# A two-block network on one core: cumulative sums in fp32r and a 512-column output product in the gated mixer

## The chip, the cores and the metric

The kernel runs on one core of a Trainium2 chip. Its engines work side by side, each through its own list of instructions in order, and wait for each other through semaphores: PE (TensorE) multiplies matrices into banks of PSUM, and PEld is its weight load, which overlaps the products; DVE (VectorE) and ACT (ScalarE) do elementwise work; POOL (GpSimd) does a little of it; SP issues the transfers. The metric is the device time of one execution in microseconds (us). The clock granted to TensorE in the profiled execution was 0.998 of full speed on average.

## The reference

`reference` runs a first block of two layers (three kinds of attention, a merge and a layer norm) on an activation of 256 tokens and 1024 features, then a second block of two layers. A layer of the second block is a gated feed-forward network, the mixer, and another feed-forward network, each behind a normalisation and with a gated residual. All is in float32. The mixer has three branches (retention, stick-breaking attention with four heads, and a state-space model) and one output product. What the change touches is this:

```
z = einsum('bhtd,bhsd->bhts', qb, kb) * scale
visible = s_pos[None, :] < t_pos[:, None]
log_beta = log_sigmoid(z)
log_keep = where(visible, log_sigmoid(-z), 0.0)
tail = cumsum(log_keep, axis=3, reverse=True) - log_keep
w = where(visible, exp(log_beta + tail), 0.0)
...
mixed = concatenate([y_ret, y_sb, y_ssm], axis=-1) @ w_out[l]     # 1536 x 1024
h = h + (1.0 + mod[:, :, 5]) * mixed
```

## The kernel before

Activations are kept with features on the 128 partitions and the 256 tokens along the row, so one feature tile is 128x256. Weights stream in as 128x1024 tiles (`raw`), through transfers that SP issues in one fixed sequence. Nearly every product keeps float32 accuracy by splitting both operands into a high and a low fp32r part. For a weight ACT makes the high part `wh` (L383) and DVE the low part `wl` (L384). For an activation ACT makes the high half (L492) and DVE the low half (L493) of one `pair` tile, which holds both side by side as 512 columns. There are two ways of adding up one 128-row step of a product:

- `mm3` (L394, L395, L396): three products of 256 columns, high weight by high half, high weight by low half, low weight by high half, all into the same 256 columns of a bank.
- `mm2` (L401, L402): the high weight over the whole pair, 512 columns, and the low weight over the high half into the second 256 columns. The result lies in two halves that have to be added when it is read.

`mm2` is used in the feed-forward down product, `mm3` in most of the rest, the mixer's output product among it.

The mixer runs twice (mixer 0 about 865 to 1045 us, mixer 1 about 1420 to 1605 us). Two of its parts matter here.

Stick-breaking: for each of the four heads, `b1` forms scores (L1814, L1815) and from them on ACT (Abs L1842, then Exp and Ln) and DVE (L1845, L1846, L1847) the logs of keeping, `k`, a 128x384 tile of type `fs`. `b2` multiplies `k` by a triangle of ones (`tri`, L1820 to L1822) to get the cumulative sums. These are plain fp32 products. DVE subtracts (L1856), ACT takes the exponential, DVE masks (L1858), and `b3` multiplies by the values. `pipeline(4, b1, b2, b3)` staggers the heads, and the pieces are mixed as side work between the `mm3` steps of the projections. A sibling of `tri`, `tri2` (L1828, L1830), takes a high and a low part as fp32r and is used by the state-space branch. Scores and cumulative sums share the two `sc` banks.

Output product: eight output tiles n of 128 features, each the sum of 12 `mm3` steps, four per branch: `YB` (stick-breaking), `YS` (state space), `YR` (retention). For n = 0 to 3 the YB and YS steps are side by side with the other branches' tails, and the YR steps come last. For n = 4 to 7 (`wide`, then `part`) the order is written out by hand (`inorder`), for the rest a scheduler orders the instructions when the program is built. `done(n)` (`resid`) then adds the tile into the residual on DVE (L1603, one instruction for every 256 columns of the bank), and `early` prepares the next normalisation: ACT makes the high half (L1495), DVE the low half (L1496), ACT the square (L1489), POOL adds the squares up (L1385). At the end PE sums the squares over the partitions (L542) inside the first product of the feed-forward network (`modhead`, 258 columns). The bank pool `mm` has four banks, and a bank of n = 0 to 3 has to be read out before `wide(4)` can write to it.

## Time and profile before

| | |
|---|---|
| time, median of 3 runs | 1797.98 us (1797.68 to 1798.31) |
| the profiled execution, its own time | 1798.37 us |
| its span, first to last instruction | 1796.6 us |
| PE busy | 1767.8 us, 98% |
| PEld busy | 1647.3 us, 92% |
| DVE busy | 1462.6 us, 81% |
| ACT busy | 1100.5 us, 61% |
| POOL busy | 190.3 us, 11% |
| share of the 16 DMA engines | 59.9% |

Shares of busy time are averages over the whole span. Products are pipelined on PE: the next starts before the one before it has ended, so what one costs is the distance from its start to the next start, not its duration. A row of the timeline gives start, duration, engine, line, operation, output and inputs; idle time ahead of it stands in brackets with the instruction that ended it.

### The profile page before, as it was taken

How to read it: one execution, taken by the hardware profiler on the slowest of the kernel's cores; microseconds unless marked ns; L12 is line 12 of the kernel's file. 1: busy time of each engine (PE TensorE's matmuls, PEld its weight loads, DVE VectorE, ACT ScalarE, POOL GpSimd, SP SyncE). 2: the span in 40 equal slices, each digit the busy share in tenths (PEclk: the TensorE clock that was granted, in tenths of full speed). 3: DMA queues.
4: the chain of work that ended last, by engine and by line, in shares of the span. 5: the costliest groups of instructions: out<-in, count | busy, mean ns of one | idle time of the engine just before them, and what ended most of it. 6: DMA issues, size and time to landing. Idle time of an engine off the chain costs nothing.

```text
span 1796.6 us, 32910 instructions
## 1 busy us (share of the span) xinstructions
PE 1767.8 (98%) x12720; PEld 1647.3 (92%) x12720; DVE 1462.6 (81%) x2893; ACT 1100.5 (61%) x2178; POOL 190.3 (11%) x205
## 2 busy tenths in 40 slices
PE   8999999999999999999999999999999999999997
PEld 8988999998899999988998998889888999899886
DVE  6787778898778789887797789697978798989774
ACT  6676555678655468674565665556555566566543
POOL 1000021300001120001114110011000104110001
PEclk9999999999999999999999999999999999999999
DMA  8755566455556655547545458585867554857761
GB/s 309 268 219 201 194 246 244 164 201 202 190 208 234 241 182 202 186 174 270 187 154 205 147 202 314 196 303 183 303 243 273 193 187 171 309 207 284 258 251 51
DMA packets 57758, 393.22 MB, mean 219 GB/s; under 512 B 6401, under 2 KB 7041, under 8 KB 15361
## 3 DMA queue, kind: packets, MB, share of 16 engines
q1 hardware_dynamic: 57600, 391.11, 59.9%
q8 instruction: 100, 1.64, 0.3%
q14 instruction: 58, 0.47, 0.1%
HBM read 390.04 MB, written 1.05 MB: 218 GB/s over the span
## 4 chain that ended last, share of the span: by engine, by line
PE 84%; DVE 8%; ACT 3%; issue 2%; DMA 2%; POOL 1%; SPq 0%; POOLq 0%; ACTq 0%; DVEq 0%
PE mm L401 21%; PE mm L394 14%; PE mm L395 14%; PE mm L396 14%; PE mm L402 11%; DVE wl L384 3%; DMA raw<-in_w 2%; DVE raw L345 2%; PE mm L445 1%; PE mm L446 1%; PE mm L447 1%; ACT wh L383 1%; PE tp L626 1%; POOL act L1395 1%; PE sc L599 0%
## 5 line engine op out<-in xcount | busy, mean ns | idle before, releaser
L383 ACT ACTIVATE wh<-raw 128x1024 fp32r<-128x1024 f32 (+2 forms) x585 | 603.0, 1036 | 446.2 <-PE mm L395 177.2
L384 DVE TENSOR_TENSOR wl<-raw,wh 128x1024 fp32r<-128x1024 f32 (+2 forms) x585 | 702.7, 1208 | 190.2 <-ACT wh L383 188.8
L394 PE MATMUL mm<-pair,wh 128*128 128x256 f32 (+2 forms) x2666 | 764.5, 287 | 6.3 <-ACT wh L383 5.2
L395 PE MATMUL mm<-pair,wh 128*128 128x256 f32 (+2 forms) x2666 | 752.6, 283 | 0.9 <-DVE pair L493 0.9
L396 PE MATMUL mm<-pair,wl 128*128 128x256 f32 (+2 forms) x2666 | 751.3, 282 | 1.0 <-DVE wl L384 0.9
L401 PE MATMUL mm<-pair,wh 128*128 128x512 f32 x1626 | 569.1, 394 | 0.0
L394 PEld LDWEIGHTS mm<-pair,wh 128*128 128x128 f32 x2666 | 504.2, 189 | 12.2 <-ACT wh L383 5.5
L395 PEld LDWEIGHTS mm<-pair,wh 128*128 128x128 f32 x2666 | 505.5, 190 | 1.8 <-DVE pair L493 1.3
L396 PEld LDWEIGHTS mm<-pair,wl 128*128 128x128 f32 x2666 | 504.9, 189 | 1.8 <-DVE wl L384 1.8
L402 PE MATMUL mm<-pair,wl 128*128 128x256 f32 x1626 | 455.6, 280 | 0.0
L401 PEld LDWEIGHTS mm<-pair,wh 128*128 128x128 f32 x1626 | 305.3, 188 | 70.9
L402 PEld LDWEIGHTS mm<-pair,wl 128*128 128x128 f32 x1626 | 306.2, 188 | 0.0
L345 DVE SCALAR_TENSOR_TENSOR raw<-raw,cond 128x1024 f32<-128x1024 f32 x160 | 194.6, 1227 | 18.0 <-DMA raw<-in_w 17.8
L1382 POOL TENSOR_TENSOR act<-act 128x256 f32<-128x256 f32 x9 | 10.8, 1200 | 563.7 <-ACT act L1489 496.6
L492 ACT ACTIVATE pair<-act 128x256 fp32r<-128x256 f32 x130 | 52.8, 411 | 27.2 <-DVE act L1673 11.7
L1385 POOL TENSOR_TENSOR act<-act 128x256 f32<-128x256 f32 x52 | 44.4, 858 | 181.3 <-ACT act L1489 172.3
L493 DVE TENSOR_TENSOR pair<-act,pair 128x256 fp32r<-128x256 f32 x130 | 56.6, 440 | 6.5 <-ACT pair L492 6.5
L304 ACT ACTIVATE fs<-fs,small 128x128 f32<-128x128 f32 x96 | 42.9, 448 | 25.6 <-DVE small L578 25.4
L445 PE MATMUL mm<-wh,pair 128*128 128x512 f32 x136 | 55.5, 408 | 0.1
L1649 DVE TENSOR_TENSOR act<-act,mm 128x256 f32<-128x256 f32 x118 | 48.8, 414 | 6.1 <-ACT act L1648 6.1
L446 PE MATMUL mm<-wl,pair 128*128 128x512 f32 x136 | 53.6, 394 | 0.0
L447 PE MATMUL mm<-wh,pair 128*128 128x512 f32 x136 | 53.6, 394 | 0.0
(304 smaller groups left out, 1686.2 us busy)
## 6 DMA issues: line engine op xcount, KB each, us to landing
raw<-in_w SPq DMA_DIRECT2D x329, 1024.0 KB, 4.8
raw<-in_w SPq DMA_DIRECT2D x32, 896.0 KB, 5.4
raw<-in_w SPq DMA_DIRECT2D x10, 512.0 KB, 4.1
tab_moba<-in_t SPq DMA_DIRECT2D x1, 1536.0 KB, 10.4
raw<-in_w SPq DMA_DIRECT2D x2, 768.0 KB, 4.8
raw<-in_w SPq DMA_DIRECT2D x3, 384.0 KB, 4.8
vt<-in_x SPq DMA_DIRECT2D x4, 256.0 KB, 6.7
out<-pair SPq DMA_DIRECT2D x4, 256.0 KB, 2.1
```

The source lines that it names most:

```text
L345: self.V.scalar_tensor_tensor(r, r, 0.5, self.cond, op0=ALU.mult, op1=ALU.mult, accum_out=self.adar[:, self.ada_n : self.ada_n + 1],)
L383: self.A.activation(h[:, :w], r, AF.Copy)
L384: self.V.tensor_tensor(l[:, :w], r, h[:, :w].bitcast(F32), op=ALU.subtract)
L394: T.matmul(ps, wh, x[0], start=first, stop=False)
L395: T.matmul(ps, wh, x[1], start=False, stop=False)
L396: self.pe = T.matmul(ps, wl, x[0], start=False, stop=last)
L401: T.matmul(ps, wh, x[2], start=first, stop=False)
L402: self.pe = T.matmul(ps[:, S:], wl, x[0], start=False, stop=last)
L445: T.matmul(ps, X[k][0][:, t], h[:, c], start=k == 0, stop=False)
L446: T.matmul(ps, X[k][0][:, t], l[:, c], start=False, stop=False)
L447: T.matmul(ps, X[k][1][:, t], h[:, c], start=False, stop=k == nk - 1)
L493: self.V.tensor_tensor(l, src, h.bitcast(F32), op=ALU.subtract)
```

## The change

Two edits in `mixer`.

In stick-breaking `tri` is gone. `b1` makes two more `fs` tiles for each head: ACT copies `k` to fp32r (`kh`), DVE subtracts it from `k` (`kl`), and `b2` calls `tri2` with the two: two products of 384 columns and two of 128, in fp32r.

In the output product `mm3` is replaced by `mm2` in `part` and in `wide`, so each tile n uses a whole bank of 512 columns, and `done` reads it with two L1603 instead of one.

In the changed kernel the lines from `tri` on have other numbers: `tri2` is L1821 and L1823, the two new instructions are L1842 (ACT) and L1843 (DVE), L1845, L1846, L1847 become L1838, L1839, L1840, L1856 and L1858 become L1852 and L1854, and L1883 becomes L1879. Lines up to L1814 keep theirs.

```diff
--- before.py
+++ after.py
@@ -1815,13 +1815,6 @@
             T.matmul(ps[:, S:384], k[:, P:S], q[:, P:S], start=True, stop=True)
             return ps[:, :384]
 
-        def tri(rhs):
-            ps = self.scb()
-            T.matmul(ps[:, S:384], self.trig, rhs[:, S:384], start=True, stop=True)
-            T.matmul(ps[:, 0:S], self.trig, rhs[:, 0:S], start=True, stop=False)
-            T.matmul(ps[:, P:S], self.ones, rhs[:, S:384], start=False, stop=True)
-            return ps[:, :384]
-
         def tri2(rs):
             ps = self.scb()
             for i, r in enumerate(rs):
@@ -1845,14 +1838,17 @@
                 V.scalar_tensor_tensor(k, z, 0.0, a, op0=ALU.max, op1=ALU.add)
                 V.scalar_tensor_tensor(a, z, 0.0, a, op0=ALU.min, op1=ALU.subtract)
                 V.tensor_tensor(k, k, LT, op=ALU.mult)
-                sbst[hh] = (a, k)
+                kh, kl = (self.fp.tile([P, 384], F32R, name="fs") for _ in range(2))
+                A.activation(kh, k, AF.Copy)
+                V.tensor_tensor(kl, k, kh.bitcast(F32), op=ALU.subtract)
+                sbst[hh] = (a, (kh, kl))
 
             return f
 
         def b2(hh):
             def f():
                 a, k = sbst.pop(hh)
-                tl = tri(k)
+                tl = tri2(k)
                 V.tensor_tensor(a, a, tl, op=ALU.subtract)
                 self.lut("ln", a, a, AF.Exp)
                 V.tensor_tensor(a, a, LT, op=ALU.mult)
@@ -2058,23 +2054,23 @@
         def part(n, Y, first=False, last=False):
             def f():
                 if first:
-                    pp[n] = self.bank()[:, :S]
+                    pp[n] = self.bank()
                 if n % 2 == 0:
                     uu[n // 2] = gen.take()
                 wh, wl = uu[n // 2]
                 for k in range(4):
                     c = slice((n % 2 * 4 + k) * P, (n % 2 * 4 + k + 1) * P)
-                    self.mm3(pp[n], wh[:, c], wl[:, c], Y[k], first and k == 0, last and k == 3)
+                    self.mm2(pp[n], wh[:, c], wl[:, c], Y[k], first and k == 0, last and k == 3)
 
             return f
 
         def wide(n):
             wh, wl = gen.take()
-            pp[n] = self.bank()[:, :S]
+            pp[n] = self.bank()
             Y2 = YB + YS
             for k in range(8):
                 c = slice(k * P, k * P + P)
-                self.mm3(pp[n], wh[:, c], wl[:, c], Y2[k], k == 0, False)
+                self.mm2(pp[n], wh[:, c], wl[:, c], Y2[k], k == 0, False)
 
         mix([part(n, YB, True) for n in range(4)], early)
         mix([part(n, YS) for n in range(4)], side[1:])
```

The change moves instructions. On PE, at the first head of stick-breaking in mixer 0, before:

```order
L396 MATMUL mm<-pair,wl 128x256
L1820 MATMUL sc<-fs,t_94 128x128
L1821 MATMUL sc<-fs,t_94 128x256
L1822 MATMUL sc<-fs,t_94 128x128
L394 MATMUL mm<-pair,wh 128x256
L395 MATMUL mm<-pair,wh 128x256
L396 MATMUL mm<-pair,wl 128x256
L1814 MATMUL sc<-pair 128x256
L1815 MATMUL sc<-pair 128x128
L394 MATMUL mm<-pair,wh 128x256
L395 MATMUL mm<-pair,wh 128x256
```

and of the changed kernel:

```order
L396 MATMUL mm<-pair,wl 128x256
L1821 MATMUL sc<-fs,tr 128x384 x2
L1823 MATMUL sc<-fs,tr 128x128 x2
L394 MATMUL mm<-pair,wh 128x256
L395 MATMUL mm<-pair,wh 128x256
L396 MATMUL mm<-pair,wl 128x256
L394 MATMUL mm<-pair,wh 128x256
L395 MATMUL mm<-pair,wh 128x256
L396 MATMUL mm<-pair,wl 128x256
L394 MATMUL mm<-pair,wh 128x256
L1814 MATMUL sc<-pair 128x256
L1815 MATMUL sc<-pair 128x128
L395 MATMUL mm<-pair,wh 128x256
```

The three fp32 products have become four fp32r products (two and two), and the next head's scores (L1814) come seven products after them instead of three.

On DVE, at the same head (`wl` is the low half of a streamed weight, L1883 and L1879 belong to the rotary tiles of the retention branch), before:

```order
L1845 SCALAR_TENSOR_TENSOR fs<-sc,fs 128x384
L1846 SCALAR_TENSOR_TENSOR fs<-sc,fs 128x384
L1847 TENSOR_TENSOR fs<-fs,tab_lt 128x384
L384 TENSOR_TENSOR wl<-raw,wh 128x1024
L1883 SCALAR_TENSOR_TENSOR pair<-fs,vt,pair 128x256
L1845 SCALAR_TENSOR_TENSOR fs<-sc,fs 128x384
L1883 SCALAR_TENSOR_TENSOR pair<-fs,vt,pair 128x256
L1846 SCALAR_TENSOR_TENSOR fs<-sc,fs 128x384
L1883 SCALAR_TENSOR_TENSOR pair<-fs,vt,pair 128x256
L1847 TENSOR_TENSOR fs<-fs,tab_lt 128x384
L1883 SCALAR_TENSOR_TENSOR pair<-fs,vt,pair 128x256
L1856 TENSOR_TENSOR fs<-fs,sc 128x384
```

and of the changed kernel:

```order
L1838 SCALAR_TENSOR_TENSOR fs<-sc,fs 128x384
L1839 SCALAR_TENSOR_TENSOR fs<-sc,fs 128x384
L1840 TENSOR_TENSOR fs<-fs,tab_lt 128x384
L384 TENSOR_TENSOR wl<-raw,wh 128x1024
L1843 TENSOR_TENSOR fs<-fs 128x384
L1879 SCALAR_TENSOR_TENSOR pair<-fs,vt,pair 128x256 x2
L1852 TENSOR_TENSOR fs<-fs,sc 128x384
L1879 SCALAR_TENSOR_TENSOR pair<-fs,vt,pair 128x256
L384 TENSOR_TENSOR wl<-raw,wh 128x1024
L1838 SCALAR_TENSOR_TENSOR fs<-sc,fs 128x384
L1854 TENSOR_TENSOR fs<-fs,tab_lt 128x384
L1839 SCALAR_TENSOR_TENSOR fs<-sc,fs 128x384
```

The low part of `k` (L1843) stands behind a `wl` of 128x1024, and the next head's first step (L1838) now comes behind this head's L1852; before it came ahead of it.

On DVE, from the last low half of the retention tiles to the readout of tile 4, in mixer 1, before:

```order
L493 TENSOR_TENSOR pair<-act,pair 128x256
L1603 SCALAR_TENSOR_TENSOR act<-mm,mod,act 128x256 x4
L1496 SCALAR_TENSOR_TENSOR pair<-act,mod,pair 128x256
L384 TENSOR_TENSOR wl<-raw,wh 128x1024
L1496 SCALAR_TENSOR_TENSOR pair<-act,mod,pair 128x256 x3
L384 TENSOR_TENSOR wl<-raw,wh 128x1024 x2
L1603 SCALAR_TENSOR_TENSOR act<-mm,mod,act 128x256
```

and of the changed kernel:

```order
L493 TENSOR_TENSOR pair<-act,pair 128x256
L1603 SCALAR_TENSOR_TENSOR act<-mm,mod,act 128x256 x6
L1496 SCALAR_TENSOR_TENSOR pair<-act,mod,pair 128x256
L1603 SCALAR_TENSOR_TENSOR act<-mm,mod,act 128x256
L1496 SCALAR_TENSOR_TENSOR pair<-act,mod,pair 128x256
L1603 SCALAR_TENSOR_TENSOR act<-mm,mod,act 128x256
L1496 SCALAR_TENSOR_TENSOR pair<-act,mod,pair 128x256
L384 TENSOR_TENSOR wl<-raw,wh 128x1024
L1496 SCALAR_TENSOR_TENSOR pair<-act,mod,pair 128x256
L384 TENSOR_TENSOR wl<-raw,wh 128x1024 x2
L1603 SCALAR_TENSOR_TENSOR act<-mm,mod,act 128x256 x2
```

The readout of tiles 0 to 3 has grown from four L1603 to eight, six of them ahead of anything else, and that of tile 4 from one to two.

## Rows read from the trace of the kernel before

**Rows 1.** The page: busy time of the engines, and the chain that ended last.
```profile
PE 1767.8 (98%) x12720; PEld 1647.3 (92%) x12720; DVE 1462.6 (81%) x2893; ACT 1100.5 (61%) x2178; POOL 190.3 (11%) x205
...
PE 84%; DVE 8%; ACT 3%; issue 2%; DMA 2%; POOL 1%; SPq 0%; POOLq 0%; ACTq 0%; DVEq 0%
```

**Rows 2.** The page, costliest groups: count, busy us, mean ns of one.
```profile
L394 PE MATMUL mm<-pair,wh 128*128 128x256 f32 (+2 forms) x2666 | 764.5, 287 | 6.3 <-ACT wh L383 5.2
...
L401 PE MATMUL mm<-pair,wh 128*128 128x512 f32 x1626 | 569.1, 394 | 0.0
...
L402 PE MATMUL mm<-pair,wl 128*128 128x256 f32 x1626 | 455.6, 280 | 0.0
```

**Rows 3.** Windows of mixer 0 and 1: busy us of each engine, clock, DMA share, GB/s.
```profile
897.00:935.00 38.00, 37.94 (x303) 37.13 (x302) 34.98 (x64) 25.59 (x49) 1.25 (x6) 1.00 0.45 158
...
1530.00:1560.00 30.00, 29.03 (x239) 27.85 (x238) 30.00 (x82) 14.98 (x43) 2.48 (x3) 1.00 0.94 358
```

**Rows 4.** Timeline of PE, cumulative sums of one head: start us, duration, instruction.
```profile
905.66 0.38 PE L1820 MATMUL sc<-fs,t 128*128 128x128 f32 x2
...
906.66 0.28 PE L395 MATMUL mm<-pair,wh 128*128 128x256 f32 x1
```

**Rows 5.** Timeline of PE, `tri2` in the state-space branch of mixer 0.
```profile
971.63 0.51 PE L1828 MATMUL sc<-fs,tr 128*128 128x384 f32 x2
...
972.33 0.28 PE L395 MATMUL mm<-pair,wh 128*128 128x256 f32 x1
```

**Rows 6.** Timeline of PE, first and last of 20 `mm3` steps in the output product.
```profile
1004.51 0.28 PE L394 MATMUL mm<-pair,wh 128*128 128x256 f32 x1
...
1011.21 0.28 PE L394 MATMUL mm<-pair,wh 128*128 128x256 f32 x1
```

**Rows 7.** Timeline of PE, `mm2` steps in the feed-forward down product, 22 steps apart.
```profile
807.12 0.40 PE L401 MATMUL mm<-pair,wh 128*128 128x512 f32 x1
807.36 0.28 PE L402 MATMUL mm<-pair,wl 128*128 128x256 f32 x1
...
814.80 0.40 PE L401 MATMUL mm<-pair,wh 128*128 128x512 f32 x1
```

**Rows 8.** Timeline of DVE at the head of rows 4.
```profile
903.48 0.55 DVE L1847 TENSOR_TENSOR fs<-fs,tab_lt 128x384 f32<-128x384 f32 x1
903.95 1.22 DVE L384 TENSOR_TENSOR wl<-raw,wh 128x1024 fp32r<-128x1024 f32 x1
905.08 0.48 DVE L1883 SCALAR_TENSOR_TENSOR pair<-fs,vt,pair 128x256 f32<-128x256 f32 x1
```

**Rows 9.** Timeline of ACT at the same head.
```profile
903.92 0.49 ACT L1842 ACTIVATE fs<-sc 128x384 f32<-128x384 f32 x1
```

**Rows 10.** Timeline of DVE, end of the output product in mixer 1.
```profile
1578.19 0.42 DVE L493 TENSOR_TENSOR pair<-act,pair 128x256 fp32r<-128x256 f32 x1
1579.20 1.66 DVE L1603 SCALAR_TENSOR_TENSOR act<-mm,mod,act 128x256 f32<-128x256 f32 x4 [0.59 <-PE mm L396]
...
1587.34 0.47 DVE L1603 SCALAR_TENSOR_TENSOR act<-mm,mod,act 128x256 f32<-128x256 f32 x1
...
1598.84 0.48 DVE L1603 SCALAR_TENSOR_TENSOR act<-mm,mod,act 128x256 f32<-128x256 f32 x1
```

**Rows 11.** Timeline of PE there: first product of `wide(4)`, and the sum of squares.
```profile
1579.74 0.39 PE L394 MATMUL mm<-pair,wh 128*128 128x256 f32 x1
...
1601.84 0.28 PE L542 MATMUL tp<-t,act 128*128 128x1 f32 x2
```

**Rows 12.** Timeline of POOL: last sum of squares of mixer 0 and of mixer 1.
```profile
1040.68 0.73 POOL L1385 TENSOR_TENSOR act<-act 128x256 f32<-128x256 f32 x1 [3.17 <-ACT act L1489]
...
1600.31 0.74 POOL L1385 TENSOR_TENSOR act<-act 128x256 f32<-128x256 f32 x1 [2.72 <-ACT act L1489]
```

**Rows 13.** Timeline of PE: the sum of squares over the partitions in mixer 0.
```profile
1043.29 0.28 PE L542 MATMUL tp<-t,act 128*128 128x1 f32 x2
```

## Prediction

> **What bounds the kernel now.** I read the page first: its busy line and chain [rows 1] show that PE works 98% of the span and makes up 84% of the chain that ended last, DVE 8%. An edit is therefore worth what it takes from PE, until PE starts to wait. The windows of the two mixers came next, since all that changes lies there: from 897 to 935 us, where mixer 0 does its stick-breaking, PE is busy 37.94 of 38.00 us with DVE at 34.98; in mixer 1, from 1530 to 1560 us, DVE is busy in all 30.00 us, the DMA engines 0.94 of the time, and PE only 29.03 [rows 3]. The clock is at its upper level (2.4 GHz) in both. So mixer 0 passes on what PE saves, while mixer 1 has a stretch between stick-breaking and output product in which DVE and the transfers may swallow it. Last I read the timelines of PE, DVE, ACT and POOL around the edits for prices and slack [rows 4 to 13], and the order of the changed kernel for what stands behind what.
>
> **The cumulative sums.** Before, `tri` starts at 905.66 and the second product behind it at 906.66 [rows 4]; taking off one ordinary distance of 0.12 us, the three fp32 products cost 0.88 us. `tri2`, which the state-space branch already uses at the same size, goes from 971.63 to 972.33 [rows 5], less 0.12 is 0.58 us. So 0.30 us for each of eight heads, 2.4 us of PE. In mixer 0 I let all 1.2 us count. In mixer 1 it may be lost in the stretch at 1530 us: between 0 and -1.2 us, and I take -0.6, since neither end has a row that favours it.
>
> What is added is on other engines: for each head a copy on ACT (0.49 us, by the same size in rows 9), hidden because ACT is busy 25.59 of 38.00 us there, and a subtraction on DVE, 0.47 us by the distance of L1847 to its successor [rows 8], 3.8 us for eight heads. DVE has 3.02 us free in that window, so four of them (1.9 us) fit on the sum; whether they fit in time depends on the place. By the order of the changed kernel the low part of `k` stands behind one `wl`. For the head of rows 4: L1847 ends at 904.03, `wl` holds DVE from 903.95 to 905.08, the subtraction would run from there to 905.63, and PE reaches the sums at 905.66. That is just in time. For the other three heads the distances are as short or a little shorter, because the next head's first step now stands behind this head's L1852: I put 0.1 us of PE wait on each, +0.3 us in each mixer, +0.6 together. The ends are 0 (cover as above) and one whole `wl`, 1.13 us, on each of eight heads, +9.0; I take a value near the lower end because the head for which there are rows lies at it. What is queued behind the waiting product on PE are `mm3` steps, which nobody needs at once, and then the next scores, whose result heads the next head's chain.
>
> **The output product.** By durations, `mm3` is three products of 0.28 to 0.29 us and `mm2` one of 0.394 and one of 0.280 [rows 2], 0.18 us less. But products are pipelined. In the output product itself 19 `mm3` steps take 1011.21 - 1004.51 = 6.70 us, 0.3526 each [rows 6]; in the down product 22 `mm2` steps take 814.80 - 807.12 = 7.68 us, 0.3491 each [rows 7]. Both move 768 columns. The saving is 0.0035 us a step, and with 8 tiles of 12 steps in two mixers, 192 steps, it is -0.7 us.
>
> The Trainium skill, TensorE: Matmul & The Clock Gate, section Back-to-back issue gap, gives a sustained 131 ns for a product of 512 columns in a stream with weight loads. Rows 7 disagree: L401 to L402 is 0.24 us. By the page the saving would be about 0.11 x 192 = 21 us (an estimate); by the row it is what stands above.
>
> **The readout of tiles 0 to 3.** A bank now holds two halves, and so 16 more L1603 run on DVE, at 0.41 us each (1.66 us for four, [rows 10]), 6.6 us. Before, in mixer 1, the last low half L493 ends at 1578.61, the first L1603 starts at 1579.20, ends at about 1579.68, and `wide(4)` starts at 1579.74 [rows 10, 11]: PE already waits for the first readout. Now the first product of a step reads both halves of the pair, so no work on the last quarter starts before L493 is through, and the bank of tile 0 is free only after its second L1603, which comes third in DVE's order (both tiles' first halves ahead): 1579.20 + 2 x 0.41 + 0.48 = 1580.50, and `wide(4)` at 1580.56. That is +0.8 us. In mixer 0 nothing waits at this place in the trace before, and the same wait may appear in part: between 0 and +0.8, I take +0.3.
>
> **The readout of tiles 4 to 7.** Here DVE and ACT work in a loop: L1603, high half, square, next `wh`, next `wl`, next L1603. In mixer 1 it goes from 1587.34 to 1598.84 in three rounds [rows 10], later than PE needs it, and its end is POOL's sum, 1600.31 to 1601.05, for which PE's L542 at 1601.84 does not wait: 0.79 us of slack [rows 11, 12]. One more L1603 in each of four tiles puts 4 x 0.41 = 1.64 us on the loop. The four extra L1603 of tiles 0 to 3 lie ahead of it, between 1579.20 and 1587.34: 8.14 us, in which DVE does four L1603 (0.41), four L1496 (0.40, as L1603) and three `wl` (1.13), 6.6 us in all. So 1.5 us are free and take in most of the other 1.64; I leave 0.5 of it. The sum comes 2.1 us later, and the slack is 0.79 and the 0.8 that `wide(4)` has lost: PE waits about 0.6 us for L542 (0 if less arrives late, 1.7 if all 3.28 do). In mixer 0 the slack is 1043.29 - 1041.41 = 1.88 us [rows 12, 13] and about 0.3 more: 2.1 - 2.2 is nothing, the upper end is 3.28 - 1.88 = 1.4, and I take +0.2.
>
> **The sum.** -1.2 - 0.6 + 0.6 - 0.7 + 0.8 + 0.3 + 0.6 + 0.2 = 0.0 us. Against the profiled execution (span 1796.6 us and 1.8 around it, 1798.37) that gives 1798.4; this execution is 0.4 above the median, so against the median the forecast is 1798.0 us: no change that can be measured (the bound is about 0.2%, 3.6 us).
>
> **Rivals.** First, PE's gain stays and the tails are hidden: the scheduler's order leaves the readouts enough room. -2.4 - 0.7 = -3.1 us, 1794.9. For it speaks mixer 0, where nothing waits at the end of the output product; against it mixer 1, where PE waits for DVE at that place already.
>
> Second, a 512-column product costs less than its columns where it stands beside the mixer's short ones, so the durations count: 0.18 x 192 = 35 us, about 1763. Rows 2 speak for it, rows 6 and 7 against it, and those are starts, which is what PE pays.
>
> Third, the other side: DVE's queue sets the pace in stick-breaking. The place is the low part of `k` behind a `wl`; it decides once that `wl` starts later than about 1.6 us ahead of PE's sums (1.13 for itself and 0.47 for the subtraction). Then each head pays up to 1.13 us: if all eight do, 9.0 - 2.4 - 0.7 + 1.9 for the tails = +7.8, 1805.8; if five do, 5.6 in place of 9.0, +4.4, 1802.4. For it speaks DVE's 34.98 of 38.00 us [rows 3] and that heads now follow each other strictly; against it that the head of rows 4 and 8 arrives in time. The Trainium skill, VectorE: DVE Perf Modes, section Rules for kernel authors, says to minimise the count of DVE operations; the change adds 24, and no run here shows yet what they cost. By that rule the change would lose.
>
> **How the numbers follow.** The forecast has a chance of 0.62, the first rival 0.19, the second 0.05, the third 0.14. The forecast's own range takes in the ends of its terms: with all of mixer 1's gain, no waits at the heads, nothing in mixer 0's tail and none at mixer 1's L542, -2.3 us; with no gain in mixer 1, the wait for `wide(4)` whole in mixer 0 too, and L542 at 1.4 and 1.7, +3.4 us. That is 1795.7 to 1801.4. The first rival and the near part of the third widen it to 1794.5 to 1802.0. Faster by over 0.2% (below 1794.4): the second rival, less than half of the first, a little of the forecast, 0.16. Slower by over 0.2% (above 1801.6): most of the third and the upper end of the forecast, 0.14. Within 0.2%: 0.70.
>
> **What would show it.** Right: the cumulative sums take 0.58 us from start to the next ordinary product, with no or short idle time ahead of the low part's product; the mixer's steps lie 0.349 us apart; a new wait of PE for L1603 at the start of `wide(4)` in mixer 1, and for L1385 or L542's input at its end; DVE's busy time up by about 10 us with the span the same. Wrong: idle time of PE for L1843 at several heads (third rival), L401 in the mixer much under 0.23 us ahead of L402 (second), or no new wait in either tail (first). A change of more than 4 us with none of these would mean that transfers moved, which I have left out because SP's list is the same in both kernels.

## The result, and the profile after

The changed kernel takes 1807.55 us (median of 4 runs, 1805.71 to 1811.43) against 1798.14 (1797.68 to 1798.76) before: 9.4 us slower, a ratio of 1.0052 with a 95% interval of 1.0041 to 1.0064. I had forecast 1798.0 and no measurable change. The profiled execution took 1808.32 us with a span of 1806.5, and a mean granted clock of 0.994 against 0.998.

The page of the changed kernel, busy time and chain, answers to [rows 1]:

```profile
PE 1771.7 (98%) x12512; PEld 1640.1 (91%) x12512; DVE 1474.0 (82%) x2917; ACT 1102.3 (61%) x2186; POOL 193.9 (11%) x205
...
PE 81%; DVE 10%; ACT 3%; issue 3%; DMA 2%; POOL 1%; POOLq 0%; DVEq 0%; ACTq 0%
```

DVE has 11.4 us more to do, where I had about 10, and so far nothing is alarming. The chain is not the same: PE's part has fallen from 84% to 81%, DVE's has risen from 8% to 10%. The list of PE's waits in both mixers (850 to 1625 us) says where:

```profile
PE sc L1821 <- POOL fs L1935: 3.7, 2, 1.9
PE tp L542 <- POOL act L1385: 3.2, 2, 1.6
PE mm L401 <- DVE pair L493: 1.9, 1, 1.9
PE tp L1403 <- DVE small L554: 1.1, 1, 1.1
PE tp L617 <- DVE fs L1854: 0.6, 2, 0.3
PE mm L401 <- DVE act L1603: 0.4, 1, 0.4
```

Columns: who waited for whom, us in total, times, the longest. Before, the second and third did not exist, and the first was shorter:

```profile
PE sc L1828 <- POOL fs L1939: 1.3, 2, 0.7
```

To see which wait reaches the end I cut both executions at the same instructions, starts of PE's sums of squares L542: the one ahead of each mixer, the one that opens its output product, the one ahead of the feed-forward network behind it, and the last of the program. The lengths of the pieces:

| piece, us | before | after | difference |
|---|---|---|---|
| start to mixer 0 | 862.52 | 861.80 | -0.7 |
| M0: mixer 0, projections and branches | 137.29 | 138.14 | +0.9 |
| O0: mixer 0, output product | 43.48 | 44.83 | +1.4 |
| F0: feed-forward networks between | 373.39 | 373.47 | +0.1 |
| M1: mixer 1, projections and branches | 137.20 | 138.63 | +1.4 |
| O1: mixer 1, output product | 47.96 | 52.94 | +5.0 |
| F1: last feed-forward network | 183.08 | 184.69 | +1.6 |
| rest | 11.7 | 12.0 | +0.3 |

The first row is code that both kernels share: mixer 0 begins between 860.4 and 866.2 us in the fourteen profiles, so times inside a mixer have to be counted from its start. Four things are in this table.

**The gain on the sums never leaves the branches.** The edit itself does what it should; PE at the head that answers to [rows 4]:

```profile
904.93 0.51 PE L1821 MATMUL sc<-fs,tr 128*128 128x384 f32 x2
905.28 0.33 PE L1823 MATMUL sc<-fs,tr 128*128 128x128 f32 x2
905.45 0.33 PE L394 MATMUL mm<-pair,wh 128*128 128x256 f32 x1
905.62 0.28 PE L395 MATMUL mm<-pair,wh 128*128 128x256 f32 x1
```

From 904.93 to 905.62, less an ordinary distance of 0.12, is 0.57 us, and no idle time: the subtraction was ready, as forecast. But PE then waits at the state-space branch, whose first sums want what POOL makes. Before:

```profile
959.26 0.33 PE L1830 MATMUL sc<-fs,tr 128*128 128x128 f32 x2
960.27 0.62 PE L1828 MATMUL sc<-fs,tr 128*128 128x384 f32 x2 [0.68 <-POOL fs L1939]
```

and after:

```profile
957.83 0.51 PE L1821 MATMUL sc<-fs,tr 128*128 128x384 f32 x2
958.18 0.33 PE L1823 MATMUL sc<-fs,tr 128*128 128x128 f32 x2
960.41 0.62 PE L1821 MATMUL sc<-fs,tr 128*128 128x384 f32 x2 [1.90 <-POOL fs L1935]
```

Counted from the start of the mixer (862.52 before, 861.80 after), the product ahead of the wait starts at 96.74 and at 96.38, so PE is 0.36 us earlier; the one behind it starts at 97.75 and at 98.61, 0.86 us later, and that is the +0.9 of M0. Of the 1.2 us saved, 0.3 had gone before, into a new wait for a head's mask (the line of L1854 above). The wait of 0.68 us was in the trace of before, at the very place that the gain had to pass, and I did not price it.

**The doubled readout delays the sum of squares in both mixers.** DVE at the end of the output product of mixer 1, which answers to [rows 10]:

```profile
1584.36 2.44 DVE L1603 SCALAR_TENSOR_TENSOR act<-mm,mod,act 128x256 f32<-128x256 f32 x6 [0.71 <-PE mm L402]
...
1593.98 0.99 DVE L1603 SCALAR_TENSOR_TENSOR act<-mm,mod,act 128x256 f32<-128x256 f32 x2
...
1607.04 1.00 DVE L1603 SCALAR_TENSOR_TENSOR act<-mm,mod,act 128x256 f32<-128x256 f32 x2
```

From the first readout to that of tile 4 it is 9.62 us (8.14 before), and the three rounds from tile 4 to tile 7 take 13.06 us (11.50 before). Two L1603 on one tile take 0.99 us, so the second starts 0.52 us behind the first, more than the 0.41 of four independent ones. POOL's last sum at that place, for [rows 12]:

```profile
1609.03 0.73 POOL L1385 TENSOR_TENSOR act<-act 128x256 f32<-128x256 f32 x1 [3.23 <-ACT act L1489]
```

and PE's sum of squares behind it, for [rows 11]:

```profile
1609.81 0.38 PE L542 MATMUL tp<-t,act 128*128 128x1 f32 x2 [1.59 <-POOL act L1385]
```

The sum ends at 1609.76 and PE, ready 1.59 us earlier, starts 0.05 later. Before, it started 0.79 us behind POOL's end without having waited [rows 11, 12].

**PE waits for the whole pair of the first retention tile.** Before, it began with the high half and waited twice, 0.5 and 0.7 us. Now it stands still from the transposes to the end of L493, 1.94 us (the bracket at the end of the second row):

```profile
1574.75 0.91 PE L1436 MATMUL tp<-t,act 128*128 128x128 f32 x3
1577.60 0.80 PE L401 MATMUL mm<-pair,wh 128*128 128x512 f32 x1 [1.94 <-DVE pair L493]
```

**The clock falls.** This I had not thought of at all. Windows of the changed kernel, mixer 1 (the granted clock is the third number from the end, 1.00 is 2.4 GHz):

```profile
1560.00:1565.00 5.00, 4.70 (x21) 4.28 (x22) 4.79 (x31) 3.01 (x13) 0.00 (x0) 0.66 0.63 216
1575.00:1580.00 5.00, 3.06 (x11) 2.31 (x11) 4.02 (x8) 3.23 (x8) 0.00 (x0) 0.74 0.97 380
1605.00:1610.00 5.00, 3.29 (x26) 3.02 (x25) 2.72 (x5) 2.63 (x4) 1.46 (x2) 1.00 0.53 197
1610.00:1615.00 5.00, 5.00 (x30) 5.00 (x30) 4.67 (x20) 2.00 (x2) 0.00 (x0) 0.66 0.27 111
```

Each low stretch lies at a standstill of PE: 1.1 us ahead of L1403 at 1560.3, 1.9 us ahead of 1577.60, 1.6 us ahead of 1609.81. In it the products of 258 columns start 0.22 us apart, where they did 0.12:

```profile
1611.61 0.42 PE L395 MATMUL mm<-pair,wh 128*128 128x258 f32 x1
1611.83 0.42 PE L396 MATMUL mm<-pair,wl 128*128 128x258 f32 x1
```

The last stretch, a mean of 0.66 over its 5 us and so some 3.4 us at half clock, is the whole +1.6 us of F1: nothing else in that feed-forward network has changed. The Trainium skill, TensorE: Matmul & The Clock Gate, section HAM oscillation — how this bites in real kernels, tells of standstills of PE, after which the array runs at half its clock. The trace agrees with the order of events, but the page's rule is for longer standstills than the 1.1 to 1.9 us here, and there the trace decides. Before, the profile of these stretches shows 1.00 throughout.

### The profile page after: what moved, and what is told of

Same layout as the page of the kernel before. It is cut to its first block, busy times and chain, and to the rows that moved or that the text cites. A ratio compares the mean times of both kernels' runs of the same rounds, so it can differ in the third digit from the quotient of the medians.

```text
span 1806.5 us, 32511 instructions
## 1 busy us (share of the span) xinstructions
PE 1771.7 (98%) x12512; PEld 1640.1 (91%) x12512; DVE 1474.0 (82%) x2917; ACT 1102.3 (61%) x2186; POOL 193.9 (11%) x205
## 4 chain that ended last, share of the span: by engine, by line
PE 81%; DVE 10%; ACT 3%; issue 3%; DMA 2%; POOL 1%; POOLq 0%; DVEq 0%; ACTq 0%
PE mm L401 22%; PE mm L394 13%; PE mm L395 13%; PE mm L396 13%; PE mm L402 11%; DVE wl L384 4%; DMA raw<-in_w 2%; ACT wh L383 1%; PE mm L445 1%; PE mm L446 1%; PE mm L447 1%; DVE raw L345 1%; PE tp L626 1%; DVE act L1603 1%; PE sc L599 0%
## 5 line engine op out<-in xcount | busy, mean ns | idle before, releaser
L394 PE MATMUL mm<-pair,wh 128*128 128x256 f32 (+2 forms) x2474 | 711.2, 287 | 5.2 <-ACT wh L383 4.6
L395 PE MATMUL mm<-pair,wh 128*128 128x256 f32 (+2 forms) x2474 | 699.4, 283 | 0.1
L396 PE MATMUL mm<-pair,wl 128*128 128x256 f32 (+2 forms) x2474 | 698.4, 282 | 0.3 <-DVE wl L384 0.2
L401 PE MATMUL mm<-pair,wh 128*128 128x512 f32 x1818 | 639.7, 396 | 2.3 <-DVE pair L493 1.9
L402 PE MATMUL mm<-pair,wl 128*128 128x256 f32 x1818 | 510.5, 281 | 0.4 <-DVE wl L384 0.4
L394 PEld LDWEIGHTS mm<-pair,wh 128*128 128x128 f32 x2474 | 468.9, 190 | 10.8 <-ACT wh L383 4.7
L395 PEld LDWEIGHTS mm<-pair,wh 128*128 128x128 f32 x2474 | 469.8, 190 | 0.8 <-DVE pair L1496 0.3
L401 PEld LDWEIGHTS mm<-pair,wh 128*128 128x128 f32 x1818 | 342.5, 188 | 81.7 <-DVE pair L493 2.3
L1385 POOL TENSOR_TENSOR act<-act 128x256 f32<-128x256 f32 x52 | 44.4, 859 | 183.1 <-ACT act L1489 174.2
L493 DVE TENSOR_TENSOR pair<-act,pair 128x256 fp32r<-128x256 f32 x130 | 56.9, 442 | 6.7 <-ACT pair L492 6.7
L445 PE MATMUL mm<-wh,pair 128*128 128x512 f32 x136 | 55.4, 408 | 0.1
L1603 DVE SCALAR_TENSOR_TENSOR act<-mm,mod,act 128x256 f32<-128x256 f32 x95 | 44.1, 479 | 12.4 <-PE mm L396 6.8
```

Source lines behind the costliest of these rows:

```text
L394: T.matmul(ps, wh, x[0], start=first, stop=False)
L395: T.matmul(ps, wh, x[1], start=False, stop=False)
L396: self.pe = T.matmul(ps, wl, x[0], start=False, stop=last)
L401: T.matmul(ps, wh, x[2], start=first, stop=False)
L402: self.pe = T.matmul(ps[:, S:], wl, x[0], start=False, stop=last)
L445: T.matmul(ps, X[k][0][:, t], h[:, c], start=k == 0, stop=False)
```

## The experiments

All times are against the kernel before, timed beside each of them on the same chip (1798.1 us beside the changed kernel, 1798.6 to 1799.1 beside the others). The pieces of the profiled execution:

| kernel | median us | ratio (95%) | M0 | O0 | F0 | M1 | O1 | F1 |
|---|---|---|---|---|---|---|---|---|
| before | | | 137.3 | 43.5 | 373.4 | 137.2 | 48.0 | 183.1 |
| changed | 1807.55 | 1.0052 (1.0041 to 1.0064) | 138.1 | 44.8 | 373.5 | 138.6 | 52.9 | 184.7 |
| `tri_only` | 1800.72 | 1.0015 (1.0006 to 1.0023) | 138.1 | 43.5 | 373.4 | 139.5* | 47.9 | 183.1 |
| `mm2_only` | 1804.92 | 1.0033 (1.0021 to 1.0045) | 137.2 | 44.8 | 375.0* | 137.2 | 52.3* | 183.2 |
| `mm2_tiles03` | 1799.38 | 1.0002 (0.9994 to 1.0011) | 137.3 | 43.2 | 373.4 | 137.3 | 50.9** | 183.1 |
| `mm2_tiles47` | 1800.39 | 1.0008 (0.9999 to 1.0017) | 137.3 | 43.4 | 373.4 | 137.2 | 49.5 | 184.7* |
| `tri_nokl` | 1799.02 | 1.0003 (0.9993 to 1.0012) | 137.0 | 43.4 | 373.4 | 137.4 | 48.4 | 183.1 |
| `tri_pool` | 1806.01 | 1.0041 (1.0027 to 1.0055) | 140.6 | 43.4 | 373.4 | 142.5 | 48.4 | 183.1 |
| `hifirst` | 1807.99 | 1.0053 (1.0038 to 1.0068) | 139.6* | 44.6 | 375.0* | 138.1 | 51.8* | 183.2 |
| `q7` | 1804.72 | 1.0029 (1.0016 to 1.0042) | 139.5* | 43.1 | 374.4 | 138.1 | 49.7 | 184.1 |
| `read_twice` | 1802.43 | 1.0020 (1.0010 to 1.0029) | 137.3 | 44.1 | 373.5 | 137.9 | 50.9 | 184.7* |
| `sub_alone` | 1802.66 | 1.0020 (1.0010 to 1.0029) | 140.2* | 43.4 | 373.4 | 140.2* | 47.0 | 183.1 |
| `masks` | 1798.19 | 0.9998 (0.9989 to 1.0008) | 137.2 | 43.5 | 373.4 | 137.9 | 48.5 | 183.1 |
| `fill` | 1805.72 | 1.0035 (1.0021 to 1.0049) | 139.5* | 44.8 | 373.5 | 138.1 | 50.9 | 183.2 |

A star is a stretch of low clock in that piece (two in O1 and one in F1 of the changed kernel, which is left unmarked). With no star a piece repeats within 0.1 us in M0 and O0 and within 0.2 in F1, so that single profiles can be compared there; M1 and O1 repeat less well: where the code is that of before, from 137.2 to 137.9 and from 47.0 to 48.5. In `q7` the cut lies at the first of four sums of squares, so some 0.9 us of its O0 and O1 stand in the next piece; its mixer 1 is also ordered otherwise, without the wait at the state-space branch.

**One edit at a time.** `tri_only` leaves the output product as it was, `mm2_only` the sums:

```diff
-                    self.mm2(pp[n], wh[:, c], wl[:, c], Y[k], first and k == 0, last and k == 3)
+                    self.mm3(pp[n], wh[:, c], wl[:, c], Y[k], first and k == 0, last and k == 3)
```

> Only the cumulative sums are changed; the output product keeps three products of 256 columns. Theory A (the gain of 0.30 us a head is lost at the state-space branch, whose first cumulative sums wait for POOL at the end of a chain through DVE and POOL, and DVE has 1.9 us more to do in each mixer ahead of it): about 1.0 us later at the end of mixer 0's branches and 1.4 us in mixer 1, 1799.5 to 1801, with PE's wait for POOL there at 1.5 to 1.9 us in each mixer against 0.7 and 0.6 before, and no other new wait. Theory B (the sums save PE what was forecast, all of the loss is in the output product): 1796 to 1797.5.

> Only the output product is changed, in all eight tiles; the cumulative sums stay in fp32. Theory A (the waits at the end of the output product and the clock that falls behind them make 7 of the 9.4 us): 1803.5 to 1807, with PE waiting 1 to 1.6 us for POOL ahead of the sum of squares in each mixer, about 1.9 us for the low half of a retention tile in mixer 1, and the granted clock under 1 in mixer 1 behind at least one of them. Theory B (the output product is all of the loss): 1807 to 1810.

Both came out as theory A has it. The sums alone cost +0.15% (2.7 us), with POOL's wait at 1.9 and 1.8 us; the output product alone +0.33% (5.9 us). Together that is 8.6 us of the 9.4. So neither edit gains anything, and the sums, on which the forecast rested, lose.

**Which part of the sums.** `sub_alone` adds the copy and the subtraction to the kernel before and uses neither; `tri_nokl` has the fp32r products and leaves the subtraction out (the low part of `k` is replaced by the high part, and each head has one `fs` tile less); `masks` takes DVE work away from the kernel before.

```diff
# sub_alone, on the kernel before
+                kh, kl = (self.fp.tile([P, 384], F32R, name="fs") for _ in range(2))
+                A.activation(kh, k, AF.Copy)
+                V.tensor_tensor(kl, k, kh.bitcast(F32), op=ALU.subtract)
                 sbst[hh] = (a, k)
# tri_nokl, on tri_only
-                V.tensor_tensor(kl, k, kh.bitcast(F32), op=ALU.subtract)
-                sbst[hh] = (a, (kh, kl))
+                sbst[hh] = (a, (kh, kh))
# masks, on the kernel before (dg: columns 0 to 127 and 256 to 383); the second mask of a head alike
-                V.tensor_tensor(k, k, LT, op=ALU.mult)
+                V.tensor_tensor(dg(k), dg(k), dg(LT), op=ALU.mult)
```

> The kernel before with two instructions a head added, the copy of k to fp32r on ACT and the subtraction on DVE, whose results nothing uses: the sums stay three fp32 products, so PE saves nothing. Theory A (DVE's load delays the chain to POOL on which the state-space branch waits): PE waits there as long as PE would be early, about 0.8 to 1.8 us in each mixer against 0.7 and 0.6 before, and the branch starts at the same time as in the kernel with the edit: 1799.5 to 1801.5. Theory D (the order of the heads, which only the fp32r sums force, delays it): 1798 to 1799.

> Only the cumulative sums are changed, and the low part of k is left out: tri2 takes the high part twice, so PE does the same four fp32r products, DVE loses the eight subtractions and each head one fs tile. Theory A (the subtraction on DVE, 0.47 us a head, delays the chain through DVE and POOL on which the state-space branch waits): the wait of PE for POOL stays but ends earlier, by most of 4 x 0.47 = 1.9 us in each mixer; 1796.5 to 1798.5. Theory D (not DVE's load, but the changed order of heads and steps delays that chain): as the kernel with the low part on DVE, 1799.5 to 1801.

> The kernel before, but the two mask products of each head in stick-breaking leave out the middle 128 of 384 columns, where the mask is 1: DVE does 256 columns in place of 384, sixteen times, about 0.1 us less each. If DVE's load ahead of the state-space branch is what PE waits for (theory A), PE's wait for POOL of 0.7 and 0.6 us shrinks and the time falls by 0.3 to 1.3 us: 1797 to 1798.3 against 1798.3 to 1799. If not (theory D), no change.

The wait for POOL, the one line of PE's waits (850 to 1625 us), of `sub_alone`:

```profile
PE sc L1828 <- POOL fs L1942: 3.7, 2, 1.9
```

and of `tri_nokl`:

```profile
PE sc L1821 <- POOL fs L1934: 2.4, 2, 1.2
```

The copy and the subtraction alone, with nothing saved on PE, lengthen the wait from 1.3 to 3.7 us and cost 0.20% (a little above the range of its expectation, by two stretches of low clock in its profile). With the copy and without the subtraction the wait is 2.4 us, and 1799.02 us lies between the ranges of the two theories, no different from before. Counted from the start of mixer 0, the state-space sums begin behind the wait at 97.75 us before, 97.43 in `tri_nokl`, 98.58 in `tri_only` and 99.25 in `sub_alone`. So DVE's subtraction puts 1.15 us (98.58 against 97.43) on the chain that ends at POOL, and the copy is not the cause. Of the 1.2 us that PE saves in mixer 0, 0.55 go into the longer wait for POOL, 0.27 into a new one at a head's scores (L1814), until DVE has read the `sc` bank, and 0.3 arrive (M0 is 137.0 against 137.3), too little to be seen in ten runs. Since a scheduler orders DVE's list anew in each kernel, what the subtraction takes and how it reorders the rest are not separated.

`masks` is a miss for theory A in its simple form: with DVE relieved, the wait stays at 1.3 us and the time does not move by what can be measured (its interval is 0.9989 to 1.0008). So DVE's load does not by itself set that wait in the kernel before. DVE's own waits from 897 to 962 us (who for whom, us, times, longest) point to what sets it before. Of the kernel before:

```profile
DVE pair L1397 <- POOL act L1395: 3.3, 6, 0.6
DVE wl L384 <- ACT wh L383: 2.8, 5, 1.5
```

and of the changed kernel:

```profile
DVE wl L384 <- ACT wh L383: 3.1, 5, 1.5
DVE pair L1397 <- POOL act L1395: 1.9, 3, 0.6
```

Before, DVE itself waits eleven times, for POOL's rotary product and for ACT's high part of the weights, so less work on it need not help. In the changed kernel three of the waits for POOL are gone, 1.4 us, less than the 1.9 us of four subtractions. That this chain through ACT and POOL sets the wait before was read, not tested.

**The subtraction on POOL** (`tri_pool`, on `tri_only`):

```diff
-                V.tensor_tensor(kl, k, kh.bitcast(F32), op=ALU.subtract)
+                G.tensor_tensor(kl, k, kh.bitcast(F32), op=ALU.subtract)
```

> Only the cumulative sums are changed, and POOL subtracts the high part from k in place of DVE. Theory A: as without the low part, if POOL is through before PE reaches the sums: 1797 to 1799; but POOL is itself in the chain of the rotary tiles and may slow DVE where both work, so up to 1800. Theory D: 1799.5 to 1801.

Both theories were too low. POOL takes 1.37 to 1.77 us for it, and PE now waits in the heads themselves (L1874 is a short memset right behind the subtraction in POOL's list):

```profile
PE sc L1821 <- POOL fs L1874: 4.7, 4, 1.4
PE sc L1821 <- POOL fs L1935: 2.3, 2, 1.2
```

**Which tiles of the output product.** `mm2` in tiles 0 to 3 or 4 to 7 only:

```diff
# mm2_tiles03 (mm2_tiles47: n >= 4, and mm2 in wide)
+                    (self.mm2 if n < 4 else self.mm3)(pp[n], wh[:, c], wl[:, c], Y[k], first and k == 0, last and k == 3)
```

> The output product is changed in tiles 0 to 3 only, cumulative sums in fp32. Theory A (two separate mechanisms: the whole pair that the first product now wants, in tiles 0 to 3, and the doubled readout that delays the sum of squares, in tiles 4 to 7): 1800 to 1802.5, with the wait for the low half of a retention tile in mixer 1 and a low clock behind it, and little or no wait ahead of the sum of squares. Theory C (the doubled readout of tiles 4 to 7 makes all of it): 1797.5 to 1799.

> The output product is changed in tiles 4 to 7 only, cumulative sums in fp32. Theory A: 1.64 us more on the loop of DVE and ACT against 1.88 and 0.79 us of slack: no wait at the sum of squares in mixer 0, 0.8 to 1.0 us in mixer 1 and, if the clock falls behind it, 1.6 us more: 1798.5 to 1800.5. Theory C (all of the loss is here): 1803 or more, with waits of about 1.6 us in both mixers.

Each half costs little (+0.02% and +0.08%, neither surely more than nothing), while both together cost +0.33%. So theory C of tiles 4 to 7 is out; the 1799.38 us of tiles 0 to 3 lie between the ranges of their two theories. In tiles 0 to 3 PE waits 1.9 us for the pair, but the sum of squares has its slack as before. In tiles 4 to 7 it waits 1.3 us in mixer 1 alone. Only with both do the delays add up to more than the slack in mixer 0 too, and 1.6 us is waited in each. With tiles 0 to 3 alone O1 is longer by 2.9 us in the profile, which has two stretches of low clock in it, and over 11 runs little of that remains.

**Readout or product.** `read_twice` is the kernel before, with every finished tile read once more; PE's list is untouched.

```diff
+                if nm.get("mix"):
+                    self.V.scalar_tensor_tensor(
+                        h[j], ps[:, a * S : a * S + S], 0.0, h[j], op0=ALU.mult, op1=ALU.add
+                    )
```

> The kernel before with one thing added: in the mixer's output product DVE reads each finished tile twice (a second L1603 with factor 0). PE's list is the one of before, three products of 256 columns and all. Theory A (the doubled readout on DVE, not the 512-column products, makes the tail of the changed kernel late): the loop of tiles 4 to 7 takes about 0.5 us more a tile, PE waits about 1.3 to 1.6 us ahead of the sum of squares in both mixers and 0.4 us or more at the start of tile 4: 1802 to 1805. Theory F (the products over the whole pair make it late): 1798 to 1800, with no wait at the sum of squares.

Theory A: +0.20%, and the wait of the changed kernel is there with `mm3` on PE. Its timeline of PE in mixer 1, the sum of squares:

```profile
1605.73 0.38 PE L542 MATMUL tp<-t,act 128*128 128x1 f32 x2 [1.51 <-POOL act L1385]
```

In mixer 0 the wait is 0.5 us (2.0 in two), less than expected. The wait at tile 4 is 0.6 us. The doubled readout makes more than half of what the output product lost, 3.6 of 5.9 us (in O0, where no clock falls, +0.7 of +1.3), without any product over a pair. What makes the rest was not separated.

**The whole pair.** `hifirst` keeps the doubled readout, but the retention steps of tiles 0 to 3 are three products again:

```diff
+                        T.matmul(pp[n][:, :S], wh[:, c], YR[k][0], start=False, stop=False)
+                        T.matmul(pp[n][:, S:], wh[:, c], YR[k][1], start=False, stop=False)
+                        self.pe = T.matmul(pp[n][:, S:], wl[:, c], YR[k][0], start=False, stop=last and k == 3)
```

> The changed kernel, but in tiles 0 to 3 the four steps over the retention tiles use three products of 256 columns into the two halves of the bank (high weight by high half, high weight by low half, low weight by high half). The readout is as in the changed kernel. Theory A (the 512-column product waits for the whole pair, before it began with the high half): the wait of 1.9 us for the low half in mixer 1 splits into shorter ones as in the kernel before (0.5 and 0.7), the clock stays at its upper level there, 1803.5 to 1806. Theory C (that wait is only brought forward, and the readout sets the end anyway): 1806.5 to 1809, with a longer wait for L1603 at the start of tile 4.

Theory C: nothing is won that four runs can show (1.0053 against 1.0052). PE's timeline in mixer 1, the first four high-half products, the first low-half product and the start of tile 4:

```profile
1582.48 0.74 PE L2064 MATMUL mm<-pair,wh 128*128 128x256 f32 x4 [0.52 <-ACT pair L492]
1583.89 0.39 PE L2065 MATMUL mm<-pair,wh 128*128 128x256 f32 x1 [0.67 <-DVE pair L493]
...
1591.19 0.50 PE L401 MATMUL mm<-pair,wh 128*128 128x512 f32 x1 [0.65 <-DVE act L1603]
```

The long wait is split as before the change, no clock falls there, and the time is waited for L1603 (0.65 us, was 0.39) and for the sum of squares. So the wait for the pair stood ahead of others that end later.

**The end of the loop, and the clock.** `q7` takes POOL's last addition out of the chain; `fill` leaves the chain alone and keeps PE busy in its wait with 13 products that nobody reads.

```diff
# q7
-        self.accum(nm["acc"], "q", q, j, not nm["fin"])
+        self.accum(nm["acc"], "q", q, j, not nm["fin"] and not nm.get("mix"))
# fill, ahead of the sum of squares
+                    fill = self.tpb()
+                    for _ in range(13):
+                        self.T.matmul(fill[:, :S], self.trigr, nm["d"][0][0][:, :S], start=True, stop=True)
```

> The changed kernel, but POOL does not add the last tile's square: PE sums it over the partitions by itself, as a second product of each column. That takes POOL's 0.74 us and two semaphores off the end of the loop of DVE and ACT and adds two small products on PE (0.45 us). Theory A (the doubled readout makes the sum of squares late in both mixers): the wait ahead of the sum of squares falls from 1.6 to 0.5 to 0.8 us in each mixer, and the clock falls less often behind it: 1803.5 to 1807. Theory E (the wait is set by something else on POOL): 1807 to 1809, with the wait unchanged.

> The changed kernel with 13 products of 256 columns, whose result nothing uses, put on PE right ahead of the mixer's sum of squares, where PE waits for POOL. Theory A (the clock falls because PE stands still there, and each fall costs 1.6 us behind it): the idle time there shrinks from 1.6 to about 0.1 us while the sum of squares starts no later, the clock stays at its upper level behind it in every profile, and the time falls by up to 3.2 us, about 1.6 in the middle: 1804.5 to 1807. Theory G (the falls have nothing to do with that wait): unchanged, 1807 to 1808.5.

`q7`: 1804.72 us, the wait down to about 0.4 us in each mixer, and no low clock behind it in its profile. `fill`: 1805.72 us. PE's timeline of `fill` in mixer 1:

```profile
1605.95 1.71 PE L1514 MATMUL tp<-pair,tr 128*128 128x256 f32 x13
1607.72 0.38 PE L542 MATMUL tp<-t,act 128*128 128x1 f32 x2
```

The sum of squares comes no earlier than POOL lets it, yet F1 is 183.2 us against 184.7 of the changed kernel, and its window behind the sum is at full clock (O1, 50.9 against 52.9, cannot be compared: in the changed kernel it holds two falls that lie ahead of this wait):

```profile
1605.00:1610.00 5.00, 4.95 (x42) 4.74 (x41) 3.15 (x20) 2.99 (x5) 0.74 (x1) 1.00 0.60 213
1610.00:1615.00 5.00, 5.00 (x45) 5.00 (x44) 5.00 (x10) 3.50 (x8) 1.09 (x2) 1.00 0.27 72
```

So a wait there can cost the wait and a fall of the clock. How often it does is read from all fourteen profiles. At the state-space branch no fall comes with the twelve waits of 0.6 or 0.7 us (six kernels) nor with the four of 1.2 us, and six come with the eleven of 1.8 or 1.9 us (six kernels); ahead of the sum of squares five with the eight waits of 1.3 to 1.6 us; at L1403 three with the ten of 1.1 us. Near 130 us, in code that no run changes, PE waits up to 2.1 us, and one fall comes with it in fourteen profiles. So the length of a standstill does not alone decide. Each fall put 1.4 to 1.6 us on its piece, where the same piece without one is there to compare. Whether one comes differs from run to run, and with it the times of the changed kernel spread over 5.7 us: its fastest run, 1805.71 us, has a clock of 0.997, its slowest, 1811.43, one of 0.993. The kernel before has such runs too: of the 29 beside `tri_only`, 1797.13 us has a clock of 0.998 and 1804.65 us one of 0.995. With five runs of `fill` (1804.12 to 1806.30 us) and four of the changed kernel, the gain of 1.8 us is not clear of that spread.

No version beat the kernel before: the median of `masks` is 0.8 us lower and that of `tri_nokl` 0.03, and both intervals hold no change.

## Why the prediction was wrong

The sum had -1.2 us for the cumulative sums with their waits and +1.2 for the output product with its readouts; alone they measured +2.7 and +5.9.

- "In mixer 0 I let all 1.2 us count." This is the step that failed first. M0 became 0.9 us longer. I took the cover from the busy share of the stretch in which the sums stand, [rows 3], and not from the next place at which PE waits for what DVE and POOL make. There PE was already 0.68 us too early. Shown by `sub_alone` (copy and subtraction alone do it) and `tri_nokl` (without the subtraction 0.3 of the 1.2 us arrive).
- The subtraction "just in time": right at the heads, no idle time at 904.93. But a cost on an engine that is 92% busy in its stretch falls due at its next deadline, which was not at the heads.
- The saving of 0.0035 us a step: of the right size. In O0, where nothing waits, `mm2_tiles03` and `mm2_tiles47` are 0.26 and 0.13 us shorter than before, 0.004 a step over 96. What the Trainium skill, TensorE: Matmul & The Clock Gate, section Back-to-back issue gap, gives for a product of 512 columns would have made it 0.11 a step (an estimate); no kernel here comes near that.
- The readout of tiles 0 to 3: the wait for L1603 appears in mixer 1 as forecast, and its size was right. In the changed kernel tile 4 starts here:

```profile
1585.77 0.47 PE L401 MATMUL mm<-pair,wh 128*128 128x512 f32 x1 [0.39 <-DVE act L1603]
```

That is 1.41 us behind the first L1603 (1584.36), and 0.54 before (1579.74 - 1579.20): +0.87, where I had +0.8. But "PE already waits for the first readout" was too strong: before, PE has no idle time there that the timeline shows. In mixer 0, where I had +0.3, no wait appeared. The wait for the whole pair, which I had named as a reason and not as a wait with a price, does not add to it as far as `hifirst` shows.
- The readout of tiles 4 to 7: the waits were 1.6 and 1.6 us, not 0.2 and 0.6. The loop and the slack were the right mechanism, two terms were too small. The larger is "So 1.5 us are free". I had taken an L1496 at 0.40 us, by L1603, and three of them take 2.73 us in that very stretch, while POOL adds squares:

```profile
1582.41 2.73 DVE L1496 SCALAR_TENSOR_TENSOR pair<-act,mod,pair 128x256 fp32r<-128x256 f32 x3
```

and on POOL:

```profile
1583.17 1.69 POOL L1385 TENSOR_TENSOR act<-act 128x256 f32<-128x256 f32 x2
```

With them DVE was busy from 1579.20 to 1587.34 without a gap, so nothing was free, and of the 1.64 us 9.62 - 8.14 = 1.48 came through, not 0.5. And a round grew by 0.52, not 0.41. `read_twice` shows the doubled readout to be the cause, `q7` that the end of this loop is what PE waits for.
- The clock had no place in the sum. Without falls the pieces add up to +0.9 and +0.9 for the branches (M1 by `fill`, `q7` and `hifirst`), +1.4 for O0 and, by `fill`, +2.9 for O1: 6.1 us. The remaining 3.3 of the 9.4 would be about two falls a run, an estimate from 1.4 to 1.6 us each. It rests on single profiles, with M1 and O1 as uncertain as said above; the share of the clock stays open within a few us.
- Of the rivals the third had the right sign and the wrong place: no head waited for the low part of `k`. The Trainium skill, VectorE: DVE Perf Modes, section Rules for kernel authors, which it named, says to keep the count of DVE operations low, and the runs agree: 24 more operations on DVE, two kinds of them measured without the rest of the change at +0.20% each.

## What to carry to other kernels

A saving on the busiest engine is worth its size only up to the next place at which that engine already waits; look for idle time behind the edit in the trace of before: here a wait of 0.7 us was the end of most of the gain. Free time on an engine is to be read from its timeline, row by row, and not from the price of one instruction elsewhere. Work given to a second engine is to be priced at that engine's next deadline, and the reader of a PSUM bank pays for a form of product that spreads its result over twice the columns. A standstill of PE cost as much again behind it, in clock, in about half of the waits of 1.3 to 1.9 us counted above, so a sum over waits should carry the clock with it.

## What the runs showed of the hardware that I had not expected

- Useless products in a wait cost nothing that shows: with 26 more products `fill` has a median of 1805.72 us against 1807.55, and F1 without the fall of the clock.
- Two DVE additions into the same tile take 0.99 us; two of the same kind into different tiles, 0.41 apart by [rows 10], would take 0.89. In the changed kernel the second reads what the first wrote.
- POOL's rotary product L1395 (128x256) takes 0.74 to 0.99 us in mixer 0 before, and in the changed kernel 1.62 to 1.64 in four of eight. POOL's timeline of the changed kernel:

```profile
931.86 0.74 POOL L1395 TENSOR_TENSOR act<-act,tab_rope 128x256 f32<-128x256 f32 x1 [9.64 <-DVE act L1394]
...
941.46 1.64 POOL L1395 TENSOR_TENSOR act<-act,tab_rope 128x256 f32<-128x256 f32 x1 [1.53 <-DVE act L1394]
...
947.90 0.98 POOL L1395 TENSOR_TENSOR act<-act,tab_rope 128x256 f32<-128x256 f32 x1 [0.22 <-DVE act L1394]
```

and DVE's:

```profile
941.28 1.20 DVE L384 TENSOR_TENSOR wl<-raw,wh 128x1024 fp32r<-128x1024 f32 x1
942.41 0.97 DVE L1396 TENSOR_TENSOR pair<-pair,tab_rope 128x256 f32<-128x256 f32 x1
...
947.86 0.43 DVE L1396 TENSOR_TENSOR pair<-pair,tab_rope 128x256 f32<-128x256 f32 x1
```

In the slow ones DVE has a `wl` between its shuffle and L1396 (941.28), and POOL ends at 943.10, 0.69 us after DVE goes on from that `wl` to L1396 (942.41), as if it had waited the `wl` out; L1396 in its turn takes 0.97, not 0.43. The Trainium skill, SBUF — State Buffer, section Who interferes with whom, says that a DVE instruction with two SBUF inputs contends with a GpSimd instruction that reads SBUF; the trace agrees. In `tri_nokl`, where no subtraction moves the `wl`, none of the eight takes over 0.98. How much of the lost time is this was not measured apart.

- The same subtraction of 128x384 takes 0.55 us on DVE (L1843 of the changed kernel) and more than twice that on POOL. POOL's timeline of `tri_pool`:

```profile
903.55 1.37 POOL L1843 TENSOR_TENSOR fs<-fs 128x384 fp32r<-128x384 f32 x1 [20.07 <-ACT fs L1842]
...
917.20 1.77 POOL L1843 TENSOR_TENSOR fs<-fs 128x384 fp32r<-128x384 f32 x1 [4.11 <-ACT fs L1842]
```
